# Seventeen groups of transposes move from TensorE to VectorE and block transfers in a two-layer hybrid trunk

## The chip, the cores and the metric

The kernel runs on one core of a Trainium2 chip. The metric is device time in microseconds, smaller is better. Three runs of the kernel before took 1862.96, 1863.21 and 1863.21 us; the median is 1863.21 us.

## The reference

Two layers, batch 1, 256 positions, 2048 channels, float32 throughout:

```
h = rms_norm(x)
proj = h @ w_in          # 2048 x 14416, split into the columns of three mixers, three gates, merge logits
y_a = latent attention(c_q, c_kv, k_rope) * silu(z_a)      # rms_norm(c_q) @ w_uq, rms_norm(c_kv) @ w_ukv, 8 heads
y_b = gelu(u_b) * (tril(w_s) . rms_norm(gelu(v_b)) + b) * silu(z_b)
y_c = gated linear attention(q_c, k_c, v_c, decay) * silu(z_c)   # 4 heads of 128, chunks of 128 positions
merged = sum over b of sigmoid(gate_b) * (y_b @ w_branch[b])
x = x + merged @ w_out
```

The linear attention needs, for each of its 2 chunks and 4 heads, attn[t,s] = sum over k of q[t,k] exp(b[t,k] - b[s,k]) k[s,k] for s <= t, where b is the running sum of the log decays.

## The kernel before

**Weights.** All matrix products go through `block` (L194) and `Weights.chunk` (L50). The weights come in 634 chunks of 512 KB (two k-tiles of 128 by 512 columns) and a few narrow ones, 320 per layer, in one fixed order. For each chunk SyncE issues a load into `wraw` (4 buffers, L64), ScalarE rounds it to `whi` (3 buffers, L65), VectorE makes the rest `wlo` = `wraw` - `whi` (3 buffers, L66), and TensorE runs 12 matmuls of 128x512: for both k-tiles and both row tiles `whi` with the high half of the activations (L207), `wlo` with the high half (L208), `whi` with the low half (L209). So ScalarE may write `whi` of chunk n only when TensorE has finished chunk n-3, VectorE follows ScalarE, and SyncE may load `wraw` of chunk n only when `wlo` of chunk n-4 is made. These three have priority over all other work in the framework's scheduler (`SPLIT_OFF`), which at build time lays out one list of instructions per engine; each engine goes through its list in order.

**Order of a layer, by chunks (counted within a layer).** 0-15 the two latents c_q, c_kv; 16-17 narrow (rotary key, decay rank); 18-33 z_a; 34-47 w_uq and w_ukv; 48-63 q and k of the linear attention; 64-79 v; 80-95 z_c; 96-111 v_b; 112-127 u_b; 128-143 z_b; 144-191 the gates of column groups 0 and 1; then merges and gates; 288-319 w_out, one block of 8 chunks for each of the four column groups of x.

**Work between the matmuls.** Generators put into `work` are advanced by `step` after every third matmul (L210), so that their TensorE instructions stand between those of the chunks.

**The two ways of turning a tensor.** The activations must stand with channels on partitions. `transpose_split` (L246) puts a generator into `work`: 8 TensorE transposes of 128x128 against the identity into two PSUM banks `ptr` (`transpose2`, L237), then `split` (L227): ScalarE writes the high half (L229), VectorE the low half (L230). `move_split` (L269) uses no TensorE: two VectorE transposes, which work within blocks of 32x32 (L277), into `part`, then 16 SyncE transfers of 32 KB (L281), each of which takes one block row to its place in `whole`, then four splits from `whole`.

Before the change `move_split` serves the branch outputs yTa, yTb, yTc (12 tensors in both layers, 192 transfers). `transpose_split` serves the latents cT (2 per layer), the merged groups mT (4 per layer) and the four groups xT of the next layer's input. In `gla` q and k of the linear attention (`qk`) are turned by `transpose2` and copied to `qkT` by ScalarE.

**Linear attention (`gla`, L614 to L706).** It forms the lower triangle level by level. `factors(lv)` makes the pair X of scaled keys and queries: four VectorE subtractions from `bT` (L653, L654), an exponential on ScalarE (L655), four VectorE multiplications with `qkT` (L657, L658). For level 0 one multiplication with k is enough (L643 and its neighbours). Then four matmuls (`plv`, L670) and two masked copies into `AT` (L679). After the eight levels come `po` (L693), the norm and `yc` (L705).

**v_b and u_b.** `gelu` (L713) takes a block's accumulators through ScalarE (L716, L719) and VectorE (L717, L718, L720); v_b is then normalised over its 1024 channels (L746).

Of the kernel before, what the change touches and what calls it, by code (L numbers as in the profile page):

```python
# [71 lines left out]
def trunk(ctx: ExitStack, tc: tile.TileContext, a, out):  # L72
# [46 lines left out]
    def gain(l, i, n=1):  # L119
        return gains[:, l, i:i + n]  # L120
# [148 lines left out]
    def move_split(src, scale, name):  # L269


        dst, part, whole = t8(name, F32R), t4("part"), t4("whole")
        dv = dst.rearrange("p (h n) -> p h n", h=2)
        blocks = part.rearrange("p (n i b) -> p n i b", n=8, i=4)
        w4 = whole.rearrange("p (n j b) -> p n j b", n=8, j=4)
        for t in range(NT):
            V.transpose(part.rearrange("p (k t c) -> p k t c", k=4, t=NT)[:, :, t, :],  # L277
                        src[:, t, :].rearrange("p (k c) -> p k c", k=4))
        for j in range(4):
            for i in range(4):  # L280
                nc.sync.dma_start(w4[32 * i:32 * i + 32, :, j, :], blocks[32 * j:32 * j + 32, :, i, :])  # L281
        for k in range(4):
            c = slice(k * S, (k + 1) * S)
            split(dv[:, 0, c], dv[:, 1, c], whole[:, c], scale(k) if callable(scale) else scale)
        return dst
# [39 lines left out]
    for l in range(DEPTH):  # L325
# [39 lines left out]
        cT = [transpose_split(cl[j], lambda k, j=j: gain(l, 16 + 4 * j + k), f"cT{j}") for j in range(2)]  # L365
# [243 lines left out]
        qkT = t8("qkT").rearrange("p (j n) -> p j n", j=2)  # L609
        S0 = t2("S0")  # L610
        yc = t8("yc").rearrange("p (t c) -> p t c", t=NT)

        def gla():
# [11 lines left out]
            for j in range(2):  # L625
                ps = [transpose2(qk[:, j], hp * 2) for hp in range(2)]
                for hp in range(2):
                    act(qkT[:, j, hp * 512:(hp + 1) * 512], ps[hp], AF.Copy)
                yield from pause(2)
# [163 lines left out]
        def merge_block(nb):  # L793
# [10 lines left out]
            mT.append(transpose_split(m, 0.5, f"mT{nb}"))  # L804
# [5 lines left out]
        merge_block(0)  # L810
        gate_block(2)
        merge_block(1)
        gate_block(3)
        merge_block(2)
        merge_block(3)
# [5 lines left out]
        for nb in range(4):  # L821
# [12 lines left out]
            if l < DEPTH - 1:  # L834
                nc.gpsimd.dma_start(rows(x1[nb]), x)
                xT.append(transpose_split(x, lambda k, l=l, nb=nb: gain(l + 1, 4 * nb + k), f"xT{nb}"))


def _lay_out(i):
# [13 lines left out]
    for l in range(DEPTH):  # L853
# [15 lines left out]
        for f, nb in ((gate, 0), (gate, 1), (branch, 0), (gate, 2), (branch, 1), (gate, 3), (branch, 2), (branch, 3)):  # L869
            f(nb)  # L870
# [54 lines left out]
```

## Time and profile before

| | |
|---|---|
| median of three runs | 1863.21 us |
| profiled execution | 1863.55 us, of which span 1861.8 us |
| granted TensorE clock | 1.00 of full speed over the execution |
| TensorE (PE) busy | 1850.6 us, 99%, 8504 instructions |
| VectorE (DVE) busy | 1107.8 us, 60% |
| ScalarE (ACT) busy | 932.2 us, 50% |
| DMA | 360.51 MB, mean 194 GB/s; 192 issues from part to whole, 32 KB each |
| chain that ended last | PE 96% (acc 90%, ptr L242 2%, plv L670 1%) |

Busy is the time in which an engine ran an instruction; the chain is followed back from the last instruction to what released it. "A <- B" in a list of waits says that A stood still until B was done.

### The profile page before, as it was taken

What the parts mean: (1) busy time and instruction counts of PE and PEld (TensorE: products, weight loads), DVE (VectorE), ACT (ScalarE), POOL (GpSimd) and SP (SyncE); (2) the same over time, 40 slices, a digit from 0 to 9 for tenths busy, and PEclk for the clock granted to TensorE, in tenths of its full rate; (3) what the DMA queues carried; (4) which work ended last, traced back from release to release, by engine and by line L of the source; (5) the groups of instructions that cost most, each with busy time, mean ns of one, the idle gap of its engine ahead of it and who ended that gap; (6) DMA issues with size and microseconds to landing.
All of it is one profiled execution on the core that took longest, in us unless ns stands there. A gap on an engine that the chain in (4) does not pass through costs nothing.

```text
span 1861.8 us, 22708 instructions
## 1 busy us (share of the span) xinstructions
PE 1850.6 (99%) x8504; PEld 1537.8 (83%) x8504; DVE 1107.8 (60%) x1436; ACT 932.2 (50%) x1174; POOL 43.6 (2%) x49
## 2 busy tenths in 40 slices
PE   8999999999999999999999999999999999999999
PEld 7888888888888888888888888888888888888887
DVE  5656558866455545465556665688664555554654
ACT  6765446554444444444547644455544444444443
POOL 0002000000000000000000010000000000000000
PEclk9999999999999999999999999999999999999999
DMA  8554564475576555575655545645755765556654
GB/s 319 188 189 156 175 209 170 147 214 183 192 209 199 192 192 192 192 235 195 212 197 185 192 146 183 205 167 158 214 176 196 211 199 190 194 187 207 220 201 158
DMA packets 150607, 360.51 MB, mean 194 GB/s; under 512 B 63456, under 2 KB 64128, under 8 KB 149984
## 3 DMA queue, kind: packets, MB, share of 16 engines
q1 hardware_dynamic: 146400, 346.30, 56.0%
q0 software_dynamic: 2656, 10.37, 1.7%
q10 hardware_dynamic: 1440, 2.39, 0.4%
q8 instruction: 66, 1.08, 0.2%
q14 instruction: 45, 0.37, 0.1%
HBM read 348.52 MB, written 4.19 MB: 189 GB/s over the span
## 4 chain that ended last, share of the span: by engine, by line
PE 96%; DVE 1%; issue 1%; ACT 1%; POOL 1%; DMA 0%; ACTq 0%; DVEq 0%
PE acc L208 30%; PE acc L207 30%; PE acc L209 30%; PE ptr L242 2%; PE plv L670 1%; DVE wlo L66 1%; PE ppv L555 1%; PE psc L524 1%; PE psc L520 1%; POOL r_q L126 1%; PE pmx L767 0%; PE po L693 0%; PE ppt L545 0%; DMA first_in<-in_gx 0%; PE accT L221 0%
## 5 line engine op out<-in xcount | busy, mean ns | idle before, releaser
L66 DVE TENSOR_TENSOR wlo<-wraw,whi 128x1024 fp32r<-128x1024 f32 (+1 forms) x642 | 782.3, 1219 | 682.2 <-ACT whi L65 681.6
L65 ACT ACTIVATE whi<-wraw 128x1024 fp32r<-128x1024 f32 (+1 forms) x642 | 677.8, 1056 | 787.0 <-PE acc L209 762.6
L207 PE MATMUL acc<-whi,xT 128*128 128x512 f32 x1792 | 704.0, 393 | 5.8 <-ACT whi L65 5.8
L208 PE MATMUL acc<-wlo,xT 128*128 128x512 f32 x1792 | 699.6, 390 | 1.5 <-DVE wlo L66 1.4
L209 PE MATMUL acc<-whi,xT 128*128 128x512 f32 x1792 | 698.6, 390 | 0.0
L207 PEld LDWEIGHTS acc<-whi,xT 128*128 128x128 f32 x1792 | 337.1, 188 | 73.7 <-ACT whi L65 5.8
L208 PEld LDWEIGHTS acc<-wlo,xT 128*128 128x128 f32 x1792 | 337.2, 188 | 71.5 <-DVE wlo L66 3.8
L209 PEld LDWEIGHTS acc<-whi,xT 128*128 128x128 f32 x1792 | 337.0, 188 | 70.0
L207 PE MATMUL acc<-whi,mT 128*128 128x512 f32 x256 | 100.0, 391 | 0.0
L209 PE MATMUL acc<-whi,mT 128*128 128x512 f32 x256 | 99.7, 389 | 0.0
L208 PE MATMUL acc<-wlo,mT 128*128 128x512 f32 x256 | 99.6, 389 | 0.0
L209 PEld LDWEIGHTS acc<-whi,mT 128*128 128x128 f32 x256 | 48.1, 188 | 10.1
L207 PEld LDWEIGHTS acc<-whi,mT 128*128 128x128 f32 x256 | 48.1, 188 | 9.8
L208 PEld LDWEIGHTS acc<-wlo,mT 128*128 128x128 f32 x256 | 48.1, 188 | 9.8
L207 PE MATMUL acc<-whi,yTa 128*128 128x512 f32 x128 | 50.0, 390 | 0.0
L209 PE MATMUL acc<-whi,yTa 128*128 128x512 f32 x128 | 49.8, 389 | 0.0
L208 PE MATMUL acc<-wlo,yTa 128*128 128x512 f32 x128 | 49.8, 389 | 0.0
L207 PE MATMUL acc<-whi,yTb 128*128 128x512 f32 x128 | 49.8, 389 | 0.0
L208 PE MATMUL acc<-wlo,yTb 128*128 128x512 f32 x128 | 49.8, 389 | 0.0
L209 PE MATMUL acc<-whi,yTb 128*128 128x512 f32 x128 | 49.8, 389 | 0.0
L207 PE MATMUL acc<-whi,yTc 128*128 128x512 f32 x128 | 49.8, 389 | 0.0
L208 PE MATMUL acc<-wlo,yTc 128*128 128x512 f32 x128 | 49.8, 389 | 0.0
(236 smaller groups left out, 1439.9 us busy)
## 6 DMA issues: line engine op xcount, KB each, us to landing
wraw<-in_w_big SPq DMA_DIRECT2D x634, 512.0 KB, 3.3
whole<-part SPq DMA_DIRECT2D x192, 32.0 KB, 3.3
x<-x POOLq DMA_DIRECT2D x8, 512.0 KB, 4.4
x<-in_x SPq DMA_DIRECT2D x2, 1024.0 KB, 8.9
wsT<-in_w_sT POOLq DMA_DIRECT2D x2, 1024.0 KB, 5.7
x<-in_x POOLq DMA_DIRECT2D x4, 512.0 KB, 5.3
out<-x ACTq DMA_DIRECT2D x8, 256.0 KB, 4.7
xTraw<-in_gx SPq DMA_DIRECT2D x3, 512.0 KB, 7.6
```

The source lines that it names most:

```text
L65: nc.scalar.activation(hi[:, c], raw[:, c], AF.Copy)
L66: nc.vector.tensor_tensor(lo[:, c], raw[:, c], hi[:, c].bitcast(F32), ALU.subtract)
L126: nc.gpsimd.tensor_tensor(r[:, :n], m[:, :n], neghalf[:, :n], ALU.pow)
L207: nc.tensor.matmul(o, xh[:, c], wh, start=kt + k == 0, stop=False)
L208: nc.tensor.matmul(o, xh[:, c], wl, start=False, stop=False)
L209: nc.tensor.matmul(o, xl[:, c], wh, start=False, stop=kt + k == kts - 1)
L242: nc.tensor.transpose(p[:, k * S + t * P:k * S + (t + 1) * P], src[:, t, (b + k) * P:(b + k + 1) * P], ident)
L520: nc.tensor.matmul(p3[:, :, 0:nk], qTr[:, c:c + P], z[:, h0 % 4:h0 % 4 + 2, 0:nk], start=True, stop=False)
L524: nc.tensor.matmul(p3[:, k, 0:nk], qTn[:, h * S + i * P:h * S + (i + 1) * P], kTn[:, h * S:h * S + nk], start=False, stop=k == 1)
L555: nc.tensor.matmul(po[:, (h - hh) * P:(h - hh + 1) * P], pT[:, k:k + P], vv[:, j, h * P:(h + 1) * P], start=j == 0, stop=j == i)
L670: nc.tensor.matmul(p[:, h * P:(h + 1) * P], X[:, 0, h, :], X[:, 1, h, :], start=True, stop=True)
```

## The change

The move (two VectorE transposes and 16 transfers) becomes a function of its own, `move`, which can write straight into a destination. `move_split` splits a tensor with one constant scale by one operation over 1024 columns in place of four over 256. Then cT (both latents, both layers), qkT (both layers, straight into `qkT`, started before `gla` is put into `work`), mT0 to mT2 (both layers) and xT0 to xT2 (between the layers) are turned by moves; mT3 and xT3 stay with TensorE. The order of merges and gates after gate 1 changes from merge 0, gate 2, merge 1, gate 3, merge 2, merge 3 to merge 0, merge 1, gate 2, merge 2, gate 3, merge 3, and the weights are laid out in that order.

```diff
+    def move(dst, src):
+        part = t4("part")
         for t in range(NT):
             V.transpose(part.rearrange("p (k t c) -> p k t c", k=4, t=NT)[:, :, t, :],
                         src[:, t, :].rearrange("p (k c) -> p k c", k=4))
+        pv = part.rearrange("p (n i b) -> p n i b", n=8, i=4)
+        dv = dst.rearrange("p (n j b) -> p n j b", n=8, j=4)
         for j in range(4):
             for i in range(4):
-                nc.sync.dma_start(w4[32 * i:32 * i + 32, :, j, :], blocks[32 * j:32 * j + 32, :, i, :])
-        for k in range(4):
-            c = slice(k * S, (k + 1) * S)
-            split(dv[:, 0, c], dv[:, 1, c], whole[:, c], scale(k) if callable(scale) else scale)
+                nc.sync.dma_start(dv[32 * i:32 * i + 32, :, j, :], pv[32 * j:32 * j + 32, :, i, :])
+    def move_split(src, scale, name):
+        dst, whole = t8(name, F32R), t4("whole")
+        dv = dst.rearrange("p (h n) -> p h n", h=2)
+        move(whole, src)
+        if callable(scale):
+            for k in range(4):
+                c = slice(k * S, (k + 1) * S)
+                split(dv[:, 0, c], dv[:, 1, c], whole[:, c], scale(k))
+        else:
+            split(dv[:, 0], dv[:, 1], whole, scale)
...
-        cT = [transpose_split(cl[j], lambda k, j=j: gain(l, 16 + 4 * j + k), f"cT{j}") for j in range(2)]
+        cT = [move_split(cl[j], lambda k, j=j: gain(l, 16 + 4 * j + k), f"cT{j}") for j in range(2)]
...
         qkT = t8("qkT").rearrange("p (j n) -> p j n", j=2)
+        for j in range(2):
+            move(qkT[:, j], qk[:, j])
...
-            for j in range(2):
-                ps = [transpose2(qk[:, j], hp * 2) for hp in range(2)]
-                for hp in range(2):
-                    act(qkT[:, j, hp * 512:(hp + 1) * 512], ps[hp], AF.Copy)
-                yield from pause(2)
...
-            mT.append(transpose_split(m, 0.5, f"mT{nb}"))
+            return m
...
         gate_block(1)
-        merge_block(0)
+        for nb in range(2):
+            mT.append(move_split(merge_block(nb), 0.5, f"mT{nb}"))
         gate_block(2)
-        merge_block(1)
+        m = merge_block(2)
         gate_block(3)
-        merge_block(2)
-        merge_block(3)
+        mT.append(move_split(m, 0.5, "mT2"))
+        mT.append(transpose_split(merge_block(3), 0.5, "mT3"))
...
-                xT.append(transpose_split(x, lambda k, l=l, nb=nb: gain(l + 1, 4 * nb + k), f"xT{nb}"))
+                turn = move_split if nb < 3 else transpose_split
+                xT.append(turn(x, lambda k, l=l, nb=nb: gain(l + 1, 4 * nb + k), f"xT{nb}"))
```

Three places in the lists of the engines follow. Line numbers of the changed kernel are a few higher (L675 is L670 of before, L662 and L663 are L657 and L658, L658 and L659 are L653 and L654, L684 is L679, L280 is L281). Numbers behind a name tell tiles of one name apart and differ between the kernels.

TensorE in the linear attention of layer 0, before: the second, third and fourth group of level matmuls, and their neighbours.

```order
L209 MATMUL acc1_2593<-whi_2753,xT2_96 128x512
L670 MATMUL plv_2770<-X_2687 128x128 x4
L207 MATMUL acc0_2592<-whi_2776,xT3_97 128x512
...
L209 MATMUL acc0_2592<-whi_2806,xT3_97 128x512
L670 MATMUL plv_2814<-X_2742 128x128 x4
L207 MATMUL acc1_2593<-whi_2806,xT3_97 128x512
```

The same of the changed kernel: chunk 111 of the layer, whose weights are whi_3125 and wlo_3126, from its second matmul to its end.

```order
L208 MATMUL acc0_2895<-wlo_3126,xT3_97 128x512
L675 MATMUL plv_2737<-X_2685 128x128 x4
L675 MATMUL plv_2774<-X_2691 128x128 x4
L675 MATMUL plv_2818<-X_2746 128x128 x4
L675 MATMUL plv_2856<-X_2790 128x128 x4
L209 MATMUL acc0_2895<-whi_3125,xT3_97 128x512
...
L209 MATMUL acc1_2896<-whi_3125,xT3_97 128x512
L675 MATMUL plv_2912<-X_2828 128x128 x4
L675 MATMUL plv_2950<-X_2866 128x128 x4
L207 MATMUL acc0_3169<-whi_3172,xT0_94 128x512
```

Before, each group of four stood between matmuls of another chunk (eight groups over chunks 100 to 110). Now four groups stand together inside chunk 111, two behind it, one in chunk 112 and one in chunk 116.

VectorE in the linear attention of layer 0, before: from the wlo of one chunk to that of the next, chunks 104 and 105.

```order
L66 TENSOR_TENSOR wlo_2860<-wraw_2858,whi_2859 128x1024
L679 COPY_PREDICATED AT_2574<-c_lvl_304,plv_2770 128x4x64 x2
L658 TENSOR_TENSOR X_2824<-X_2824,qkT_2577 128x32x8
L657 TENSOR_TENSOR X_2824<-X_2824,qkT_2577 128x32x8
L658 TENSOR_TENSOR X_2824<-X_2824,qkT_2577 128x32x8
L654 TENSOR_TENSOR X_2880<-bT_2576 128x64x4
L653 TENSOR_TENSOR X_2880<-bT_2576 128x64x4
L654 TENSOR_TENSOR X_2880<-bT_2576 128x64x4
L66 TENSOR_TENSOR wlo_2895<-wraw_2893,whi_2894 128x1024
```

The same of the changed kernel from chunk 111 on: wlo_3126 is that of chunk 111, wlo_3173 of chunk 112, wlo_3191 of chunk 113.

```order
L66 TENSOR_TENSOR wlo_3126<-wraw_3124,whi_3125 128x1024
L66 TENSOR_TENSOR wlo_3173<-wraw_3171,whi_3172 128x1024
L648 TENSOR_TENSOR X_2685<-X_2685,qkT_2585 128x512
L662 TENSOR_TENSOR X_2691<-X_2691,qkT_2585 128x4x64
L662 TENSOR_TENSOR X_2746<-X_2746,qkT_2585 128x8x32
L662 TENSOR_TENSOR X_2790<-X_2790,qkT_2585 128x16x16
L66 TENSOR_TENSOR wlo_3191<-wraw_3189,whi_3190 128x1024
L662 TENSOR_TENSOR X_2790<-X_2790,qkT_2585 128x16x16
L684 COPY_PREDICATED AT_2582<-c_lvl_304,plv_2774 128x4x64 x2
L684 COPY_PREDICATED AT_2582<-c_lvl_304,plv_2818 128x4x2x32 x2
```

The multiplications with the turned k (L648, L662) now stand behind the wlo of chunk 112. From there to the wlo of chunk 115 VectorE's list holds the rest of seven levels: 1 of L648, 19 of L662 and L663, 16 of L658 and L659, 12 masked copies, six gelu operations of v_b's first half, and the wlo of chunks 113 and 114. The 16 transfers of k are issued one or two per chunk, the last behind the load of chunk 114.

SyncE at the end of layer 0, before: there are loads only from the moves of yTc and yTb on to those of yTa in layer 1.

```order
L64 DMA wraw<-in_w_big 128x1024
L281 DMA whole<-part 32x8x32 x2
L64 DMA wraw<-in_w_big 128x1024 x141
L64 DMA wraw<-in_w_small 128x768 x2
L64 DMA wraw<-in_w_big 128x1024 x53
L281 DMA whole<-part 32x8x32 x3
```

The same of the changed kernel at chunks 329 to 334 (320 is the first of layer 1); these are transfers of xT2.

```order
L64 DMA wraw<-in_w_big 128x1024
L280 DMA whole<-part 32x8x32
L64 DMA wraw<-in_w_big 128x1024
L280 DMA whole<-part 32x8x32 x7
L64 DMA wraw<-in_w_big 128x1024 x4
L280 DMA whole<-part 32x8x32
```

The last seven transfers of xT2 stand behind the load of chunk 330. On ScalarE the splits of xT2 stand behind the whi of chunk 326. TensorE uses xT2 first in chunk 324.

## Rows read from the trace of the kernel before

**Rows 1.** The waits of TensorE over the whole execution: who waited, for whom, then microseconds in total, how many times, and the longest.

```profile
PE acc L207 <- ACT whi L65: 5.8, 1, 5.8
PE acc L208 <- DVE wlo L66: 1.4, 4, 0.4
```

**Rows 2.** The groups of TensorE instructions by line and shape, the transposes of the tensors that the diff names: busy time and mean ns of one, and after the bar the idle time before them.

```profile
L242 PE MATMUL ptr<-c_ident,merged 128*128 128x128 f32 x64 | 8.3, 272 | 0.0
...
L242 PE MATMUL ptr<-c_ident,x 128*128 128x128 f32 x32 | 4.1, 272 | 0.0
L242 PE MATMUL ptr<-c_ident,qk 128*128 128x128 f32 x32 | 4.1, 272 | 0.0
L242 PE MATMUL ptr<-c_ident,cq 128*128 128x128 f32 x32 | 4.1, 272 | 0.0
```

**Rows 3.** The chain of waits in order of time: start, length and what it was; one group of eight transposes, and one of eight level matmuls of the linear attention.

```profile
53.72 0.87 PE ptr L242 x8
...
315.37 0.89 PE plv L670 x8
```

**Rows 4.** The timeline of TensorE from 45 to 70 us: start, time to the end, instruction. A matmul starts before the one before it has ended, so the distance between starts is its price.

```profile
44.99 0.39 PE L207 MATMUL acc<-whi,xT 128*128 128x512 f32 x1
...
51.56 0.39 PE L209 MATMUL acc<-whi,xT 128*128 128x512 f32 x1
...
53.56 1.03 PE L242 MATMUL ptr<-c_ident,cq 128*128 128x128 f32 x8
...
54.55 0.28 PE L222 MATMUL accT<-xT,whi 128*96 128x256 f32 x1
```

**Rows 5.** The waits of ScalarE for a free weight buffer, and SyncE's for the refilling, over the whole execution: total, times, longest (the first from the list of all waits, the second from SyncE's own).

```profile
ACT whi L65 <- PE acc L209: 762.6, 481, 4.4
...
SPq L64 <- DVE wlo L66: 1313.3, 584, 8.7
```

**Rows 6.** The timeline of all engines at 346 us: one round of the weight buffers, from the last matmul of a chunk over ScalarE to VectorE. In brackets the idle time before, and who ended it.

```profile
346.62 0.39 PE L209 MATMUL acc<-whi,xT 128*128 128x512 f32 x1
...
347.10 1.06 ACT L65 ACTIVATE whi<-wraw 128x1024 fp32r<-128x1024 f32 x1 [1.65 <-PE acc L209]
...
348.19 1.23 DVE L66 TENSOR_TENSOR wlo<-wraw,whi 128x1024 fp32r<-128x1024 f32 x1 [1.15 <-ACT whi L65]
```

**Rows 7.** The groups of VectorE instructions by line and shape, those of the linear attention and of the gelu (columns as in rows 2).

```profile
L679 DVE COPY_PREDICATED AT<-c_lvl,plv 128x256 f32<-128x256 int32 x28 | 13.4, 532 | 0.0
...
L657 DVE TENSOR_TENSOR X<-X,qkT 128x256 f32<-128x256 f32 x28 | 11.5, 422 | 0.0
L718 DVE TENSOR_TENSOR g<-g,acc 128x512 f32<-128x512 f32 x16 | 10.9, 684 | 0.2
...
L746 DVE SCALAR_TENSOR_TENSOR vn<-vn,rvh,vg 128x1024 f32<-128x1024 f32 x4 | 5.1, 1282 | 0.1
...
L643 DVE TENSOR_TENSOR X<-X,qkT 128x512 f32<-128x512 f32 x2 | 1.4, 688 | 0.0
```

**Rows 8.** The timeline of VectorE in the linear attention of layer 0, 339 to 345 us, where it runs without a gap. Between the first two rows stand five more of the first one's length.

```profile
339.74 0.43 DVE L657 TENSOR_TENSOR X<-X,qkT 128x256 f32<-128x256 f32 x1
...
341.76 1.22 DVE L66 TENSOR_TENSOR wlo<-wraw,whi 128x1024 fp32r<-128x1024 f32 x1
342.90 0.42 DVE L654 TENSOR_TENSOR X<-bT 128x256 f32<-128x256 f32 x1
343.23 1.32 DVE L679 COPY_PREDICATED AT<-c_lvl,plv 128x256 f32<-128x256 int32 x2
344.44 0.43 DVE L657 TENSOR_TENSOR X<-X,qkT 128x256 f32<-128x256 f32 x1
```

**Rows 9.** The timeline behind the linear attention of layer 0, 350 to 375 us: a norm that goes from VectorE over GpSimd and back, and the first ScalarE operation of a gelu.

```profile
354.16 0.17 DVE L124 TENSOR_SCALAR m_o<-sso 128x4 f32<-128x4 f32 x1 [0.91 <-ACT junk L698]
...
355.55 0.23 DVE L702 TENSOR_SCALAR ror<-r_o,r_x 128x4 f32<-128x4 f32 x1 [1.22 <-POOL r_o L126]
...
358.22 0.69 ACT L716 ACTIVATE g<-acc,r_x 128x512 f32<-128x512 f32 x1
```

**Rows 10.** The timeline of SyncE's queue at 212 us, where the block transfers of yTa are issued among the weights: start, length of the run of issues, count.

```profile
215.28 0.55 SPq L64 DMA_DIRECT2D wraw<-in_w_big  x1
215.87 1.89 SPq L281 DMA_DIRECT2D whole<-part  x3
```

**Rows 11.** The last row of the view of the tile whole (time from issue to landing of its 192 block transfers, all of them of branch outputs), and from the groups of ScalarE the split of xT from PSUM.

```profile
DMA to landing us min/median/max: 1.9/3.3/8.0
...
L229 ACT ACTIVATE xT<-ptr,first_in 128x256 fp32r<-128x256 f32 x16 | 7.1, 475 | 3.1 <-DVE xT L230 3.0
```

**Rows 12.** Two stretches: from:to, length, busy time (and count) of PE, PEld, DVE, ACT and POOL, the granted clock, the share of the DMA engines, GB/s. In the first, 19 block transfers of yTa are issued; the second has weights alone.

```profile
212.00:240.00 28.00, 28.00 (x136) 23.45 (x135) 15.96 (x20) 11.74 (x12) 0.54 (x1) 1.00 0.74 224
620.00:700.00 80.00, 80.00 (x355) 66.26 (x354) 37.77 (x32) 34.60 (x36) 0.00 (x0) 1.00 0.55 192
```

**Rows 13.** The timeline of TensorE at the start of the program, after its first wait. Eleven matmuls start before the third row.

```profile
5.85 1.22 PE L207 MATMUL acc<-whi,xT 128*128 128x512 f32 x2 [5.85 <-ACT whi L65]
...
10.28 0.63 PE L208 MATMUL acc<-wlo,xT 128*128 128x512 f32 x1
10.71 0.44 PE L209 MATMUL acc<-whi,xT 128*128 128x512 f32 x1
...
11.21 0.39 PE L208 MATMUL acc<-wlo,xT 128*128 128x512 f32 x1
```

More of the change, by code (lines that the diff above doesn't have):

```diff
@@ L267, in transpose_split @@
         return dst
[L269 to L275, printed above, removed]
+    def move(dst, src):
+        part = t4("part")
         for t in range(NT):
@@ L868, in _lay_out @@
         branch = lambda nb: [put(g["w_branch"][l, b][:, nb * 512:(nb + 1) * 512]) for b in range(3)]
-        for f, nb in ((gate, 0), (gate, 1), (branch, 0), (gate, 2), (branch, 1), (gate, 3), (branch, 2), (branch, 3)):
+        for f, nb in ((gate, 0), (gate, 1), (branch, 0), (branch, 1), (gate, 2), (branch, 2), (gate, 3), (branch, 3)):
             f(nb)
```

## The prediction

> **What bounds the kernel now.** I read TensorE's waits first: it waits 5.8 us once, at the start, and 1.4 us in four pieces after that [rows 1]. So TensorE is the bound from end to end, and every microsecond taken from its list is a microsecond of the kernel, as long as the others keep feeding it. Then the price of a matmul: 29 starts from 44.99 to 51.56 us are 0.2266 us each, so one chunk (12 matmuls) is 2.72 us [rows 4]. Then how far the others are ahead. ScalarE waits 481 times for TensorE to free a weight buffer, SyncE 584 times for VectorE [rows 5]: the feeding engines have slack, but the three buffers let them run at most three chunks ahead. From the start of a chunk's last matmul to its end one price passes; 0.25 us later ScalarE begins, VectorE 1.09 us after that and needs 1.23 [rows 6]. So a wlo is ready 2.6 us after TensorE has freed its buffer, and other work may delay it by two chunks less that, some 5.6 us, before TensorE stands still. That lead is the cover which every edit below uses.
>
> **What goes.** Groups of eight transposes: 4 for cT, 4 for qk, 6 of 8 for mT, 3 of 4 for xT, 17 in all, out of 20 that the four rows show [rows 2]. A group holds TensorE 0.87 us on the chain [rows 3]; in the timeline, from 53.56 to 54.55, 0.99 us pass for a group and one 256-wide matmul, half of 0.2266, which gives 0.87 to 0.88 [rows 4]. 17 x 0.875 = 14.9 us. It ends the matter if all moves are hidden.
>
> **What is added and moved.** 34 VectorE transposes and 272 block transfers in SyncE's queue. The moves that stand two chunks ahead of their use (cT0, mT0 to mT2, xT0, xT1) I cost at nothing: yTb and yTc are turned so in the kernel before, and TensorE's list of waits has no entry for them [rows 1]. If that cover fails in one, it costs a landing, 2 to 8 us [rows 11]. Three places stand worse in the order.
>
> *The linear attention, per layer.* k's transfers trickle out with the loads, the last behind that of chunk 114, and the multiplications with k stand behind wlo of chunk 112. From there to the end of wlo of chunk 115 VectorE must do 1 + 19 + 16 + 12 + 6 operations and three wlo. Start to start, six 256-wide operations take 2.02 us (0.337 each), a wlo 1.14, two masked copies 1.21 [rows 8], and the masked copies have a mean of 0.53 [rows 7]; between 0.53 less an overlap of 0.085 and half of 1.21 I take 0.5. That is 0.60 for L648 (0.688 less the overlap of 0.085 that 0.422 and 0.337 show), 19 x 0.335 = 6.4, 16 x 0.335 = 5.4, 12 x 0.5 = 6.0, four gelu operations at 0.60 and two at 0.34 = 3.1, three wlo = 3.4: 24.8 us; by full durations (0.69, 0.42, 0.53, 0.68, 1.22 [rows 7, 8]) it is 29.0. TensorE has in the same stretch four chunks, 10.9 us, and seven level groups at 0.89 [rows 3], 6.2: 17.1. TensorE cannot go round it: the first four level groups stand inside chunk 111 and need those multiplications, and the list of VectorE makes wlo of 114 and 115 wait for the rest. In the kernel before, the same work lay one group per chunk over eleven chunks. So TensorE stands still for 24.8 - 17.1 = 7.7 us; walking the groups one by one I get 7.9, which I take.
>
> After it the lead is gone, and the gelu and normalisation of v_b come late. Let T be the end of chunk 119. wlo of 122 is made at T + 2.6; behind it the last gelu of v_b (0.42 + 0.68, a tanh of 0.69 and a hand-over of 0.2, 0.68), a square on ScalarE with its hand-over (0.9), the sum, a norm that goes to GpSimd and back (1.39 from 354.16 to 355.55, and 0.4 for its ends), one operation of u_b (0.42), two of 1.28, and wlo of 123 (1.23) [rows 7, 9]: T + 12.2. TensorE has three chunks and the first matmuls of the fourth to do, 8.4 us. It waits 3.8 there, part of it for the accumulators of v_b's second half, which that gelu frees. Some 0.9 more I give to yc's norms in chunks 118 and 119, which cost nothing in the kernel before only because the lead was full. Together 12.6 us per layer; layer 1 has the same order: 25.2 us. Bounds: 2 x 7 if the tail finds a lead again, 2 x 20 with full durations throughout and both tails.
>
> *xT2 at the layer boundary.* TensorE needs it in chunk 324. Its splits stand on ScalarE behind whi of 326, which waits for the end of chunk 323; its last seven transfers stand behind the load of 330, which waits for wlo of 326. So nothing can be early. From the end of 323: 2.6 to wlo of 326, a load issue of 0.59, six spacings of 0.65 ((1.89 - 0.585) / 2 for three issues) [rows 6, 10], which brings the last issue to 7.1; a landing of 1.9 at least [rows 11], and one split of 0.475 [rows 11]: 9.5, with hand-overs 9.7 us of TensorE idle. The bounds are 8 (the last blocks are needed only for the second k-tile) and 13 (the median landing, 3.3, and a wait in SyncE's queue). I take 9.7. In the kernel before the same place costs one transpose group.
>
> *cT1 in layer 0* has its last transfer behind the load of chunk 39 and its use in chunk 40; three operations on VectorE stand behind its split. 1 us, between 0 and 2.
>
> *The clock after a long stand.* At the start, after 5.85 us of idle, eleven matmuls start in 4.86 us, 0.43 to 0.44 apart, and then 0.25 [rows 13]: 4.86 - 11 x 0.2266 = 2.4 us. The only wait of that length that I forecast is xT2's; 2.2 us, between 0 and three times that (once more in each layer's linear attention). The Trainium skill, page "TensorE: Matmul & The Clock Gate", section "HAM oscillation — how this bites in real kernels", says that gaps in which TensorE idles bring the array back to half its clock. The start agrees in the spacing, 0.43 against 0.227, though the granted clock of the trace reads 1.00 there.
>
> **Sum**, on the profiled execution (1863.55 us, its span of 1861.8 and 1.75 around it; 0.3 above the median of the runs, which is no difference): 1863.55 - 14.9 + 25.2 + 9.7 + 1.0 + 2.2 = 1886.8, so **1887 us**.
>
> **Rivals.**
>
> 1. *The lead covers the burst and xT2 after all* (faster). For it: SyncE and ScalarE have hundreds of waits to spare, and the twelve moves of the kernel before are free [rows 1, 5]. Against it: the engines would have to leave the printed order, or VectorE to run its list well under the start-to-start times. Then 1863.55 - 14.9 = 1848.7 us. It decides as soon as all stands together stay under 14.9 us. The Trainium skill, same page, section "Architectural detail: the array is 16× 32×32, not 1× 128×128", says that ScalarE and VectorE take their queue strictly in order and that only TensorE may pull a weight load ahead. By that rule this rival falls and the sum stands at 1887; VectorE's rows at 339 to 345 us agree, standing in the printed order [rows 8].
> 2. *Only xT2 costs* (same). VectorE's burst is hidden because TensorE's own level groups and the slack of 5.6 us take up 7.7. For it: the shortfall is only a little above the slack. Against it: the lead is already spent, since the work begins behind wlo of 112 while TensorE is in 111. 1863.55 - 14.9 + 9.7 + 1 + 2.2 = 1861.6 us.
> 3. *Heavier* (slower still): full durations (29.0 - 17.1 = 11.9 in place of 7.9) in both layers, the median landing for xT2 (+1.4), and the half-rate start after each stand (+4.4): 1887 + 8 + 1.4 + 4.4 + about 4 for the tails = 1905 us.
> 4. *The DMA engines fill up* (far slower). While yTa's 19 transfers are issued, their share is 0.74, against 0.55 with loads alone [rows 12]: 0.19 x 28 / 19 = 0.28 us of all engines for each transfer, 76 us for 272. It costs only where the share reaches 1; with two tensors in flight at once it comes near 0.8. 1863.55 - 14.9 + 76 = 1925 at worst.
>
> **How the numbers follow.** The forecast 0.74, rival 1 0.07, rival 2 0.06, rival 3 0.11, rival 4 0.02. The forecast's own range is 1871 to 1905, from 2 x 7 with 8 for xT2 and no clock loss (1863.55 - 14.9 + 14 + 8 = 1871) to rival 3. To leave out no more than 2 in 10, the range reaches down to rival 2 and a little past rival 3: 1862 to 1908. What can be told from no change is 0.2%, 3.7 us: faster is below 1859.5, which is rival 1 and a little of rival 2, 0.09; same, the rest of rival 2, 0.06; slower 0.85.
>
> **What would show it.** TensorE's list of waits should have, in each layer, level matmuls waiting for X on VectorE, some 8 us, and further waits for wlo and the vn operations, some 4; at the boundary one wait of nearly 10 us of L207 for the split of xT2; 8368 TensorE instructions, 136 fewer. VectorE should run without a gap for some 25 us there, SyncE should issue seven transfers in a row. The forecast is wrong if TensorE's waits stay under 15 us in sum, if X's multiplications come before wlo of 112, if xT2 has landed when chunk 324 begins, or if the waits fall on the mT or cT moves, which I put at nothing and 1 us.

## The result and the profile after

| | before | after |
|---|---|---|
| median | 1863.17 us (1862.96 to 1863.21, 4 runs) | 1890.5 us (1889.25 to 1892.84, 4 runs) |
| ratio, with 95% interval | | 1.0148 [1.0131, 1.0166] |
| profiled execution, span | 1863.55, 1861.8 us | 1890.12, 1888.3 us |
| TensorE instructions | 8504 | 8368 |
| mean granted clock | 1.000 | 0.992 |

The change is 27.3 us slower, 3.5 us more than forecast. The lines of the page of the changed kernel that answer to the table of before are the busy times and the chain that ended last (share of the span by engine).

```profile
PE 1850.7 (98%) x8368; PEld 1531.0 (81%) x8368; DVE 1126.0 (60%) x1440; ACT 925.7 (49%) x1136; POOL 43.6 (2%) x49
...
PE 90%; DVE 5%; DMA 2%; issue 1%; ACT 1%; POOL 1%; SPq 0%; ACTq 0%; DVEq 0%; POOLq 0%
```

136 instructions are gone and TensorE is busy for just as long (1850.6 us before): instructions that run at half rate count as busy too, so the busy time hides both the gain and part of the loss (a matmul lasts 0.63 us in place of 0.39 in the slow stretch shown below for xT2). The chain shows it better: VectorE and DMA are now on it with 7%, before with 1%. The waits of TensorE over the whole execution, as in [rows 1]:

```profile
PE acc L207 <- ACT xT L229: 9.4, 1, 9.4
PE plv L675 <- DVE X L663: 9.0, 4, 2.9
PE acc L207 <- ACT whi L65: 5.7, 1, 5.7
PE acc L207 <- DVE sza L427: 3.6, 2, 3.1
PE acc L207 <- DVE vn L725: 3.3, 4, 1.2
PE acc L208 <- DVE wlo L66: 2.3, 7, 0.4
```

Two lines had been there, the first chunk's wait for whi and the small ones for wlo. Four are new, 25.3 us in sum, and each names its place: xT2 at the layer boundary, the level matmuls, the gating products of z_a (sza), and the gelu of v_b (vn). The list has one more new entry, of 0.2 us.

What a place costs in all, waits, slow matmuls and saved transposes together, comes out of the two traces when the start of the same weight matmul (the n-th of 7728) is compared in both. The difference after minus before changes by more than 0.3 us for good only here; steps of 0.3 us at the start and at the end, and smaller ones, make 0.6 us together.

| stretch | difference moves by | transposes saved in it | so the place costs |
|---|---|---|---|
| layer 0, up to the end of z_a | -1.4 us | 1.8 us | 0.4 us |
| layer 0, from the end of z_a into w_uq and w_ukv | +7.1 | 0 | 7.1 |
| layer 0, linear attention to the first gates | +8.2 | 1.8 | 10.0 |
| mT0 to mT2 in both layers, xT0 to xT2: nine steps | -0.9 each | 0.9 each | 0 |
| layer boundary, where xT2 is needed | +12.7 | 0 | 12.7 |
| layer 1, latents | -1.4 | 1.8 | 0.4 |
| layer 1, linear attention to the first gates | +8.9 | 1.8 | 10.7 |

In the linear attention one group of matmuls of the position mixing (pmx) stands 47 us earlier than before (402.4 against 449.0 us in layer 0); the stretch is taken so long that it lies inside in both.

The four waits are 25.3 us and these places 41.3. The rest lies in TensorE's busy time, matmuls at half rate among it; it was not taken apart further.

**xT2.** The timeline of the changed kernel at the boundary: TensorE's matmuls (and one some way behind them), ScalarE's splits, SyncE's last run of transfers.

```profile
954.88 0.39 PE L209 MATMUL acc<-whi,xT 128*128 128x512 f32 x1
964.69 0.80 PE L207 MATMUL acc<-whi,xT 128*128 128x512 f32 x1 [9.42 <-ACT xT L229]
...
969.54 0.63 PE L209 MATMUL acc<-whi,xT 128*128 128x512 f32 x1
969.97 0.58 PE L207 MATMUL acc<-whi,xT 128*128 128x512 f32 x1
970.38 0.40 PE L208 MATMUL acc<-wlo,xT 128*128 128x512 f32 x1
```

```profile
955.35 1.06 ACT L65 ACTIVATE whi<-wraw 128x1024 fp32r<-128x1024 f32 x1 [1.66 <-PE acc L209]
964.12 1.71 ACT L229 ACTIVATE xT<-whole,first_in 128x256 fp32r<-128x256 f32 x4 [7.72 <-DMA whole<-part]
```

```profile
957.69 0.33 SPq L64 DMA_DIRECT2D wraw<-in_w_big  x1
958.07 4.50 SPq L280 DMA_DIRECT2D whole<-part  x7
```

The steps are to be read one by one: whi of chunk 326 starts 0.25 us behind the last matmul's slot, the load of 330 goes out at 957.69, seven transfers follow, the split begins at 964.12, TensorE goes on at 964.69. Behind the stand matmuls start 0.43 us apart until 969.97, twelve of them, as after the first wait of the program [rows 13]. The clock of that stretch, and of the two other slow ones, in the view of stretches (columns as in [rows 12]; cT1, linear attention, xT2):

```profile
106.00:114.00 8.00, 6.76 (x16) 4.88 (x17) 4.02 (x8) 2.68 (x5) 0.00 (x0) 0.57 0.19 67
...
357.00:363.00 6.00, 4.77 (x20) 4.26 (x20) 6.00 (x17) 4.06 (x6) 0.00 (x0) 0.52 0.28 90
...
965.00:971.00 6.00, 6.00 (x16) 4.67 (x16) 3.01 (x8) 3.15 (x8) 0.00 (x0) 0.55 0.00 0
```

The granted clock is half, 1.2 GHz, in most of each. Here the column does show what at the start it does not.

**Linear attention.** VectorE's timeline of the changed kernel in layer 0: the wlo of chunk 112, the first multiplication with k, the one wait in the stretch, and three wlo in a row (115 to 117) at its end. Then TensorE's: the first matmul of chunk 110, the level groups, the first of chunk 115.

```profile
345.68 1.23 DVE L66 TENSOR_TENSOR wlo<-wraw,whi 128x1024 fp32r<-128x1024 f32 x1 [1.50 <-ACT whi L65]
346.83 0.68 DVE L648 TENSOR_TENSOR X<-X,qkT 128x512 f32<-128x512 f32 x1
...
367.94 1.32 DVE L684 COPY_PREDICATED AT<-c_lvl,plv 128x256 f32<-128x256 int32 x2 [0.99 <-PE plv L675]
...
370.09 3.86 DVE L66 TENSOR_TENSOR wlo<-wraw,whi 128x1024 fp32r<-128x1024 f32 x3
```

```profile
344.39 0.39 PE L207 MATMUL acc<-whi,xT 128*128 128x512 f32 x1
...
347.66 3.81 PE L675 MATMUL plv<-X 128*128 128x128 f32 x32
...
356.67 2.05 PE L675 MATMUL plv<-X 128*128 128x128 f32 x8 [2.88 <-DVE X L663]
359.95 2.05 PE L675 MATMUL plv<-X 128*128 128x128 f32 x8 [1.23 <-DVE X L663]
...
371.38 0.61 PE L207 MATMUL acc<-whi,xT 128*128 128x512 f32 x2
```

From 346.83 to the end of wlo of 115, 1.2 us after 370.09, are 24.5 us, of which VectorE itself stands 0.99 for the matmuls of the seventh group. The first four groups run through in 3.81 us; TensorE stands before the fifth and the sixth, which then take 2.05 us each for eight matmuls (the seventh group, from 366.85 us on, takes 1.05). From 361.65 to 371.38 it runs without a stand.

**cT1.** At the end of z_a in layer 0, TensorE's and VectorE's timelines of the changed kernel:

```profile
103.21 0.39 PE L209 MATMUL acc<-whi,xT 128*128 128x512 f32 x1
106.69 0.68 PE L207 MATMUL acc<-whi,cT 128*128 128x512 f32 x1 [3.10 <-DVE sza L427]
...
109.63 0.80 PE L207 MATMUL acc<-whi,cT 128*128 128x512 f32 x1 [0.55 <-DVE sza L427]
```

```profile
104.72 1.23 DVE L66 TENSOR_TENSOR wlo<-wraw,whi 128x1024 fp32r<-128x1024 f32 x1 [1.49 <-ACT whi L65]
105.87 0.68 DVE L427 SCALAR_TENSOR_TENSOR sza<-th,acc 128x512 f32<-128x512 f32 x1
107.30 1.68 DVE L230 SCALAR_TENSOR_TENSOR cT<-whole,first_in,cT 128x256 fp32r<-128x256 f32 x4 [0.75 <-ACT cT L229]
108.90 1.88 DVE L427 SCALAR_TENSOR_TENSOR sza<-th,acc 128x512 f32<-128x512 f32 x3
```

All four products sza stand around the split of cT1. TensorE waits not for cT but for accumulators: the first block of w_uq writes into the banks of z_a's first half, which the first two products free. The first stands behind wlo of chunk 36, and that wlo cannot be made before TensorE has ended chunk 33. The second stands behind the split of cT1.

### The profile page after: what moved, and what is told of

Same layout as the page of the kernel before. It is cut to its first block, busy times and chain, and to the rows that moved or that the text cites. A ratio compares the mean times of both kernels' runs of the same rounds, so it can differ in the third digit from the quotient of the medians.

```text
span 1888.3 us, 22818 instructions
## 1 busy us (share of the span) xinstructions
PE 1850.7 (98%) x8368; PEld 1531.0 (81%) x8368; DVE 1126.0 (60%) x1440; ACT 925.7 (49%) x1136; POOL 43.6 (2%) x49
## 4 chain that ended last, share of the span: by engine, by line
PE 90%; DVE 5%; DMA 2%; issue 1%; ACT 1%; POOL 1%; SPq 0%; ACTq 0%; DVEq 0%; POOLq 0%
PE acc L208 29%; PE acc L209 29%; PE acc L207 29%; DVE wlo L66 2%; DMA whole<-part 1%; PE plv L675 1%; PE ptr L242 1%; PE ppv L563 1%; PE psc L532 1%; PE psc L528 1%; POOL r_q L126 1%; DVE yc L710 0%; ACT whi L65 0%; PE pmx L772 0%; PE ppt L553 0%
```

## The experiments

The ratios are to runs of the kernel before on the same chip; its medians there were 1862.95 to 1863.73 us. The expectations put the linear attention at 22.5 us for both layers, read over a stretch that ends before the pmx matmuls; over the stretches of the table it is 20.7. Two theories stand against each other in the first four: three places in the order cost everything, or every added transfer costs its share.

**q and k by TensorE again**

```diff
-        for j in range(2):
-            move(qkT[:, j], qk[:, j])
...
+            for j in range(2):
+                ps = [transpose2(qk[:, j], hp * 2) for hp in range(2)]
+                for hp in range(2):
+                    act(qkT[:, j, hp * 512:(hp + 1) * 512], ps[hp], AF.Copy)
+                yield from pause(2)
```

> The changed kernel with q and k of the linear attention turned by TensorE again, as before; all else as changed. Theory (three places in the order cost, the rest is gain): in the trace of the changed kernel the linear attention took 10.9 us more in layer 0 and 11.6 us more in layer 1 than in the kernel before, apart from the 2 x 1.8 us that the removed transposes save; without the move 1890.5 - 22.5 + 3.6 = about 1872 us, TensorE's waits for X gone, level groups one per chunk. Rival (the loss comes from the number of block transfers, whatever their place): 64 of 272 added transfers go, 64/272 of a loss of 27.3 us is 6.4 us, about 1884 us.

Measured: 1872.5 us (1871.26 to 1875.68), ratio 1.0056 [1.004, 1.0071]. TensorE's waits for X and vn are gone from its list:

```profile
PE acc L207 <- ACT xT L229: 9.3, 1, 9.3
PE acc L207 <- ACT whi L65: 5.9, 1, 5.9
PE acc L207 <- DVE sza L427: 4.2, 2, 3.1
```

The theory of places holds for the largest term.

**xT2 by TensorE again**

```diff
-                turn = move_split if nb < 3 else transpose_split
+                turn = move_split if nb < 2 else transpose_split
```

> The changed kernel with xT2 turned by TensorE again (xT0 and xT1 stay moved). Theory: the stand of 9.4 us at the layer boundary and the slow matmuls behind it go, 12.7 us between the same matmuls of the two kernels, less 0.9 us for the transposes that return: 1890.5 - 11.8 = about 1879 us. Rival (number of transfers): 16 of 272, 1.6 us, about 1889 us.

Measured: 1879.0 us (1878.6 to 1882.91), ratio 1.009 [1.0076, 1.0104]. The line of xT is gone, the other places stay (sza with 5.7 us in place of 3.6; the profiled execution is the slowest of the four). One tensor of 17 carries 11.5 us net, so the loss does not go by number.

**The latents by TensorE again**

```diff
-        cT = [move_split(cl[j],
+        cT = [transpose_split(cl[j],
```

> The changed kernel with the latents cT of both layers turned by TensorE again. Theory: the stand behind z_a in layer 0 and the slow matmuls behind it, 7.1 us, go, and four groups of transposes return, 3.6 us: about 1887 us; the two gating products of z_a's first half stand early again on VectorE. Rival (number of transfers): 64 of 272, 6.4 us, about 1884 us.

Measured: 1885.8 us (1885.64 to 1887.13), ratio 1.0123 [1.0109, 1.0137]; the line of sza is gone. By time alone it stands between the two theories; the wait that went speaks for the first. The latents are worth 4.7 + 3.6 = 8.3 us by this run; by the table it is 0.4 + 7.1 + 0.4 = 7.9.

**All three by TensorE again**

The three edits above together; mT0 to mT2, xT0 and xT1 stay moved.

> The changed kernel with qk, xT2 and cT all turned by TensorE again: only mT0 to mT2, xT0 and xT1 are moved, in the new order of merges. Theory: no stand is left and eight groups stay saved at 0.9 us: 1863.2 - 7.2 = about 1856 us, clear of 1863.2. Rival (number of transfers): 128 of 272 added transfers remain, a loss of 12.8 us, about 1876 us.

Measured: 1857.6 us (1856.28 to 1857.88), ratio 0.9968 [0.9956, 0.9981]. The median is 1.6 us above the forecast. It is faster than the kernel before with 128 of the 272 added transfers, and TensorE's list of waits is that of before but for 0.5 us:

```profile
PE acc L207 <- ACT whi L65: 5.7, 1, 5.7
PE acc L208 <- DVE wlo L66: 1.7, 5, 0.4
PE plv L678 <- DVE X L666: 0.2, 1, 0.2
```

So the number of transfers is not the cause. The next runs ask what makes the three places bad: the turning itself, or the queue that it goes through.

**q's and k's transfers issued by GpSimd**

```diff
-    def move(dst, src):
+    def move(dst, src, q=nc.sync):
...
-                nc.sync.dma_start(dv[32 * i:32 * i + 32, :, j, :], pv[32 * j:32 * j + 32, :, i, :])
+                q.dma_start(dv[32 * i:32 * i + 32, :, j, :], pv[32 * j:32 * j + 32, :, i, :])
...
-            move(qkT[:, j], qk[:, j])
+            move(qkT[:, j], qk[:, j], nc.gpsimd)
```

> The changed kernel, with the 64 block transfers of q and k issued by GpSimd in place of SyncE; nothing else is changed by hand. In the order the level groups then stand one per chunk again, over chunks 99 to 112. Theory (the transfers come late because they trickle behind the weight loads in SyncE's queue): the stands of both layers' linear attention go, 22.5 us, about 1868 us. Rival (turning by transfers is late whatever issues it, since 32 transfers in a row have to land before the first level): VectorE waits for them in chunk 99 and TensorE stands as long as before, 1885 to 1895 us.

Measured: 1871.8 us (1869.17 to 1871.96), ratio 1.0039 [1.0025, 1.0054]. It misses the 1868 by 4 us and the rival by 13; in its trace no wait for X or vn is left. The stretch in which the changed kernel stood, here:

```profile
340.00:372.00 32.00, 31.84 (x153) 26.41 (x152) 26.41 (x53) 18.73 (x36) 2.04 (x2) 1.00 0.36 124
```

TensorE is busy for 31.84 of 32 us at full clock. So neither turning q and k by VectorE nor the landing of block transfers as such made it slow. What the edit changes is two things at once: the queue, and with it the order in which the lists are laid out, where the level groups stand one per chunk again. This holds for every run with GpSimd's queue below; the two are not told apart. The missing 4 us, by the starts of the weight matmuls: 1.8 are the expectation's 22.5 in place of 20.7; the linear attention still costs 0.6 and 0.7 us in the two layers; and layer 0 up to there is 1.0 us worse than in the changed kernel (at the end of z_a the difference moves by 9.1 us in place of 7.1).

**q's and k's moves ahead of everything, still by SyncE**

```diff
-            move(qkT[:, j], qk[:, j])
+            with tc.high_priority(offset=2 * SPLIT_OFF):
+                move(qkT[:, j], qk[:, j])
```

> The changed kernel, with the moves of q and k put ahead of everything else, so that SyncE issues their 32 transfers in a row without a weight load between; level groups over chunks 99 to 108. Theory: the stands of the linear attention go (22.5 us), but 32 issues at 0.62 us hold SyncE's queue for 20 us, and the next weight load comes later than TensorE can bear (the slack between a load's normal issue and its use is about 16.3 - 2.6 - 3.3 - 2.3 = 8 us): a stand of about 12 us in each layer in its place, 1890.5 - 22.5 + 25 = about 1893 us, with TensorE waiting for whi and wlo, and these for wraw. Rival (the queue has time enough, the order of the list alone was bad): about 1868 us.

Measured: 1889.2 us (1888.33 to 1891.11), ratio 1.0139 [1.0124, 1.0154], 4 us below the theory and clear of the rival, but the wait that appears is another one. SyncE's queue, ScalarE's next weights and TensorE's new wait:

```profile
282.88 20.85 SPq L280 DMA_DIRECT2D qkT<-part  x32
```

```profile
308.00 1.06 ACT L65 ACTIVATE whi<-wraw 128x1024 fp32r<-128x1024 f32 x1 [1.93 <-DMA wraw<-in_w_big]
```

```profile
PE plv L676 <- DVE X L650: 15.2, 2, 7.6
```

SyncE is held for 20.85 us and the next weights are there at 309 us, as forecast. TensorE stood already, since its list now has the first level group before those weights and waits for X at that group. Both ends fall together, so the run gives the price (over the stretches of the table the difference to the kernel before moves by 8.6 us in layer 0 and 7.6 in layer 1, against 8.2 and 8.9 in the change) but does not say which of the two alone would set it. What it shows: put ahead of everything, the 32 transfers hold SyncE's queue for 20.85 us, and q and k are about as dear as behind the loads.

**xT0 to xT2 issued by GpSimd**

`move` with the argument `q` as above.

```diff
-    def move_split(src, scale, name):
+    def move_split(src, scale, name, q=nc.sync):
...
-        move(whole, src)
+        move(whole, src, q)
...
-                xT.append(turn(x, lambda k, l=l, nb=nb: gain(l + 1, 4 * nb + k), f"xT{nb}"))
+                scale = lambda k, l=l, nb=nb: gain(l + 1, 4 * nb + k)
+                xT.append(move_split(x, scale, f"xT{nb}", nc.gpsimd) if nb < 3 else transpose_split(x, scale, f"xT{nb}"))
```

> The changed kernel, with the 48 block transfers of xT0 to xT2 issued by GpSimd. The splits of xT2 then stand behind whi of chunks 320 and 321 in place of 326, ahead of TensorE's use in 324. Theory (xT2 was late only by its place in SyncE's queue): the stand and the slow matmuls behind it go, 12.7 us, about 1878 us, and xT2 stays moved. Rival (a block of x is turned too late by any queue, one block being 8 chunks or 21.8 us): TensorE waits for xT again, above 1886 us.

Measured: 1881.8 us (1879.2 to 1884.01), ratio 1.0097 [1.0082, 1.0112]. In its profile (1879.2 us) the line of xT is gone, and the difference at the layer boundary moves by 0.3 us in place of 12.7. The median is 4 us above the forecast; the profiled execution is the fastest of four, so what the others lost is not seen.

**The latents issued by GpSimd**

The same edit of `move_split`, with `nc.gpsimd` for cT.

> The changed kernel, with the 64 block transfers of the latents cT issued by GpSimd. In the order the gating products of z_a's first half then stand behind wlo of chunks 28 and 31 in place of 36, and the splits of cT1 behind whi of 24. Theory (layer 0's stand behind z_a comes from products that hold accumulators and stand behind a split that waits for late transfers): the 7 to 9 us there go, 1882 to 1884 us. Rival (the stand comes from the moves' own work on VectorE and ScalarE): TensorE still waits for sza, about 1890 us.

Measured: 1883.5 us (1882.07 to 1891.79), ratio 1.0105 [1.0089, 1.012]. The median is the forecast's. The profiled execution is the slowest, the one of 1891.79. At the end of z_a nothing is lost in it, but TensorE stands some chunks earlier, and the difference moves by +7.0 us up to there, where 1.8 were to be saved:

```profile
PE pk L401 <- ACT kr L404: 4.2, 1, 4.2
```

ScalarE's splits of cT1, which stand ahead of kr in its list, and GpSimd's last transfers of cT1 and load of b_a:

```profile
77.58 1.31 ACT L229 ACTIVATE cT<-whole,first_in 128x256 fp32r<-128x256 f32 x3 [4.87 <-DMA ba<-in_b_a]
```

```profile
61.46 8.10 POOL L280 DMA_DIRECT2D whole<-part  x14
71.38 1.15 POOL L280 DMA_DIRECT2D whole<-part  x2 [1.82 <-DMA whole<-part]
...
73.05 0.58 POOL L389 DMA_DIRECT2D ba<-in_b_a  x1
```

The view names b_a as what the splits waited for, but they do not read it, and it landed 5.4 us after its issue, at 78.5, when the first split had begun. What they read is the 16 blocks: the last was issued at 71.96 and landed at 77.51. So in this execution the moved latents are late by GpSimd's queue too: it began at 61.46 and stood 1.82 us for the landing of an earlier transfer before the last two. The other four executions (1882.07 to 1885.48) have no trace.

**Cause by cause removed, everything kept moved**

cT, q and k, and xT0 to xT2 issued by GpSimd; mT and the branch outputs by SyncE.

> The changed kernel, with the block transfers of cT, q and k, and xT0 to xT2 issued by GpSimd (176 of the 272 added ones); mT and the branch outputs stay with SyncE. Theory (the moves are worth their 17 groups of transposes if nothing comes late, the three places being all that costs): 1863.2 - 17 x 0.9 = about 1848 us, with no wait of TensorE over 1 us but the first. Rival (GpSimd's issues or the transfers cost something of their own): between the 1857.5 us of the version with only mT, xT0 and xT1 moved and 1863.

Measured: 1851.6 us (1850.29 to 1853.88), ratio 0.9937 [0.9924, 0.9949], the fastest kernel of the study: 38.9 us below the change with the same 8368 TensorE instructions. Its page and TensorE's waits:

```profile
PE 1836.2 (99%) x8368; PEld 1522.5 (82%) x8368; DVE 1125.9 (61%) x1440; ACT 926.1 (50%) x1136; POOL 145.4 (8%) x225
```

```profile
PE acc L207 <- ACT whi L65: 6.0, 1, 6.0
PE pk L401 <- ACT kr L404: 1.6, 1, 1.6
PE acc L208 <- DVE wlo L66: 1.3, 4, 0.4
PE ptr L242 <- DVE x L834: 0.6, 1, 0.6
```

TensorE's busy time falls by 14.4 us (1850.6 to 1836.2), which is the saving that the change meant. VectorE does the same work as in the change (1125.9 and 1126.0 us). It misses 1848 by 3.7 us, of which the two new lines are 2.2; it is clear of the rival's 1857.5. By the starts of the weight matmuls the moves still cost about 1 us in layer 0's latents, 0.6 in each layer's linear attention and 0.9 at the boundary.

**Layer 0's latents by TensorE, the rest as above**

```diff
-        cT = [move_split(cl[j],
+        cT = [(transpose_split, move_split)[l](cl[j],
```

(layer 1's latents by SyncE)

> The changed kernel, with the transfers of q and k and of xT0 to xT2 issued by GpSimd, and the latents of layer 0 alone turned by TensorE again (layer 1's stay moved, by SyncE). Theory: 15 groups of transposes stay saved and nothing stands: 1863.2 - 15 x 0.9 = about 1850 us, level with or 1 to 2 us below the version in which GpSimd moves the latents too (1851.6), since layer 0's latents there make TensorE wait some 2 us for late landings. Rival (that version's missing 4 us are lost elsewhere): 1853 us or more.

Measured: 1853.4 us (1851.34 to 1860.99), ratio 0.9953 [0.9938, 0.9969]. It is not below the version before it, and its runs scatter more, so the expected 1 to 2 us are not there; by its number the rival holds. In its profile the wait for kr is gone and one of 1.9 us for x stands there:

```profile
PE ptr L242 <- DVE x L834: 1.9, 2, 1.4
```

```profile
926.74 0.51 ACT L229 ACTIVATE xT<-whole,first_in 128x256 fp32r<-128x256 f32 x1 [3.72 <-DMA x<-in_x]
```

```profile
930.57 0.68 DVE L834 TENSOR_TENSOR x<-x,acc 128x512 f32<-128x512 f32 x1
```

x is the sum of the fourth column group, and it stands on VectorE behind the splits of xT2. Here too the view names a load (x, from GpSimd's queue) that landed at 927.94, when the first split had begun; the last block transfer of xT2, which the split reads, was issued by GpSimd at 921.56 and landed at 926.52. So the 1.9 us are again a moved tensor that comes late.

**The new order of merges alone**

No added move; the new order of merges, gates and weights, and the constant-scale split in one operation.

```diff
-            mT.append(move_split(merge_block(nb), 0.5, f"mT{nb}"))
+            mT.append(transpose_split(merge_block(nb), 0.5, f"mT{nb}"))
```

> The change's new order of merges and gates, with the weights in that order, and the constant-scale split in one operation, but no added move: cT, qk, mT and xT all by TensorE as before. Theory (the order only makes room for mT's moves): within 1 us of 1863.2. Rival (two merges side by side leave VectorE and ScalarE behind, and part of the loss is theirs): 1865 us or more.

Measured: 1863.2 us (1862.89 to 1864.07), ratio 0.9998 [0.999, 1.0007]. The order costs nothing by itself.

## Why the prediction was right, point by point

- **The direction and its mechanism** were right: TensorE's list is the kernel, the moves take 17 groups off it, and what they put into the three-chunk lead of the feeding engines costs more. In sum, by the table of places: 1863.55 - 15.3 + 20.7 + 12.7 + 7.1 + 0.8 = 1889.55, and the profiled execution took 1890.12; the 0.6 left are the small steps. The total is nearer than its terms: cT1 cost 6.1 us more than forecast and the linear attention 4.5 less, so part of the agreement is luck.
- **The saving**, 17 x 0.875: the difference falls by 0.90 for each moved mT and for xT0 to xT2. 15.3 in place of 14.9.
- **No cost for the moves with two chunks ahead**: right for mT and xT0, xT1, and nearly so for cT0 and layer 1's latents (0.4 us each). The run with all three places undone confirms it as a whole.
- **VectorE's stretch**: forecast 24.8 us, measured 24.5. That is nearer than the working: the twelve masked copies took 4.5 us from start to start in place of 6.0, and the 0.99 us in which VectorE stood were not forecast. TensorE needs 19.8 us for chunks 110 to 114 and seven groups (5 x 2.72 + 7 x 0.89); in the trace 27.0 us pass from the start of chunk 110 to that of 115 in layer 0 (344.39 to 371.38) and 27.7 in layer 1, so 7.2 and 7.9 us are lost, against 7.9. Where in the stretch TensorE stands was wrong: I had it stand at the first level group, while four groups ran through and it stood at the fifth and sixth. The waits for X are 9.0 us over both layers, where I had put some 8 in each; the rest is time in which TensorE counts as busy. That the length of VectorE's list alone sets the loss is argued, not shown: wlo of 115 is at its end, made at 371.3, but TensorE came to chunk 115 just then, and its list has no long wait for a wlo.
- **The tail behind it**: forecast 4.7 us a layer, measured 10.0 - 7.2 = 2.8 and 10.7 - 7.9 = 2.8. This term was too long; the waits for vn, which I had put at 3.8 a layer, are 3.3 over both.
- **xT2**: forecast a stand of 9.7, measured 9.4, by the steps that the prediction lists: the last of the seven transfers is issued by 962.6 (958.07 + 4.50) and the split begins at 964.12.
- **The clock term**, 2.2 us once, has the right price and the wrong count: twelve matmuls at 0.43 cost 2.4 us behind xT2, and about 2.4 more behind cT1, where the stand was only 3.1 us. In the linear attention the clock falls too (0.52 over 357 to 363 us), though the working counted no clock there beside a stand of 7.9 us (only its upper bound did). What it costs was not tried apart: behind the fifth group TensorE waits for X in any case, but behind the slow sixth VectorE stands 0.99 us for the seventh, so about 1 us may be the clock's.
- **The step that failed** is "cT1 in layer 0 has its last transfer behind the load of chunk 39 and its use in chunk 40; three operations on VectorE stand behind its split. 1 us, between 0 and 2." It cost 7.1, with a wait of TensorE for sza of 3.6 us, although a sign of being wrong that the prediction names is waits that fall on the cT moves. I read the three operations as work that delays a split. They are products that free accumulators, as is one more that stands ahead of the split, and chunk 34 needs those. The first stands behind a wlo that cannot be made before chunk 33 has ended, the same pattern that I had priced for xT2, and the others behind a split that waits for the last transfer. In the total this is hidden: the linear attention, forecast at 25.2, took 20.7.
- **The rivals.** "The lead covers it" falls with four new waits; its time, 1848.7 us, is nearly reached by the version with GpSimd's queue, so it names what the moves are worth. "Only xT2 costs" falls with the run that undid q and k. "Heavier" falls in its largest terms: VectorE's stretch is 24.5 us and not 29.0, and the tail is 2.8 us a layer; its half-rate matmuls did come in the linear attention, but their price lies inside the 7.2 and 7.9 us. "The DMA engines fill up" falls with the version of 1851.6 us, which has all 272 transfers.
- **The order of the lists.** [rows 8] are of chunks behind the list that is printed for the kernel before, so they cannot show that VectorE kept to it; the printed part itself ran in its order from 321.13 to 324.94 us. In the changed kernel the first multiplication with k ran behind wlo of chunk 112 (346.83 after 345.68), the splits of xT2 behind whi of 326 (964.12 after 955.35). The Trainium skill, page "TensorE: Matmul & The Clock Gate", section "Architectural detail: the array is 16× 32×32, not 1× 128×128", states that VectorE and ScalarE take their queues strictly in order. These traces agree with it.

## What to carry to other kernels

Work that left a full engine was paid here in the queues that feed that engine: count what the move adds to each in-order list, ask how far ahead of its user it ends, and look for instructions that stand behind a buffer which the user itself has to free, since such a stand can be worked out from the lists: xT2's was forecast to 0.3 us, while cT1's was missed because its products were not read so. When an operation moves in an engine's list, ask what it frees as well as what it makes. Before giving up such a move, try another queue for its transfers: here that, with the lists laid out anew for it, turned 27 us lost into 12 us won. Then look at what that queue delays in its turn: the last microseconds here were again moved tensors that came late.

## What was not expected of the hardware

- The half-rate matmuls came not only behind the long stand. Behind 3.1 us (cT1, granted clock 0.57 over 106 to 114 us) they cost about 2.4 us, as much as behind 9.4. Stands of nearly one length did not fare alike: behind 2.88 us in layer 0's linear attention the eight level matmuls took 2.05 us, behind 2.90 us in layer 1's 1.26 (at 1297.17 us), and only the next group took 2.05.
- TensorE's busy time is the same with 136 instructions fewer (1850.6 and 1850.7 us), and shows the whole saving only without the stands: 1836.2 us with all 17 groups moved, 1843.2 with the eight of mT, xT0 and xT1.
- GpSimd issued block transfers with no wait of TensorE from them in the linear attention (64 of them). At the boundary (48) TensorE waited 0 to 1.9 us, and for layer 0's latents 1.6 and 4.2 us. In the two executions in which the view of waits names a small load of the same queue (b_a, x), the landing times show that it was the last block transfer.
